# Modulation sums of the first feed-forward: one vector operation per eighth of a weight piece, fed by four one-chunk buffers

## The chip, the core and the metric

The kernel runs on one core of a Trainium2 chip. The core has a matrix engine (TensorE, PE in the profile; its weight loads are listed apart as PEld), a vector engine (VectorE, DVE), a scalar engine (ScalarE, ACT), a general engine (GpSimd, POOL) and a queue engine (SyncE, SP) that issues all DMAs of this kernel. They run side by side, each strictly in the order of its own instruction list, and wait for one another through semaphores. Data lie in SBUF and in HBM; products of PE land in PSUM, which has eight banks here, split in three pools ("a" four, "b" three, "c" one).

The metric is device time in microseconds (us), the median of several executions. The kernel before takes 3250.4 us (3247.34 to 3251.12, three runs).

## What is computed

The kernel is one layer of a diffusion backbone over 256 latent and 256 context tokens of width 2048. What matters here is the modulation and the first feed-forward step:

```
mod   = (silu(c)     @ w_ada + b_ada)      # 18432 columns for the latent stream
mod_c = (silu(c_ctx) @ w_ada + b_ada)      # and the same for the context stream
# x += 1/2 * gate * SwiGLU(modulate(RMSNorm(x)))  for both streams, width 5632 inside
h = _modulate(_rmsnorm(x, gain), m[:, 0], m[:, 1])
return x + HALF_STEP * m[:, 2] * _swiglu(h, w_gate, w_up, w_down)
```

After it come an input projection, a state-space scan, a Hyena branch, a merge and a second feed-forward, which use further columns of the same modulation. All of it is in float32; a product is made of three passes, with each operand split in a high part (the cast to the PE's own format) and a low part (the rest).

## The kernel before

The first feed-forward treats the 5632 inner columns in 22 blocks of 256. A block has six weight pieces of 1 MB: gate, up, gate, up (each 8 chunks of 128 rows by 256 columns, `gate_up`), then the down product of the block before in two pieces (`down` inside `ffn1`). Every piece costs PE 48 products of 128 x 512. `wpiece` prepares one: a DMA into `raw` (three buffers), a cast on ACT into the high part `wh` (two buffers), and two subtractions on DVE into the low part `wl` (two buffers). The `wh` of a piece can be written only when PE has done with the piece two earlier. The products of `down` go through PSUM into the running sums `xl` and `xc` by two DVE operations for each of 16 tiles (`evac1`), and between them stands the chain SiLU on ACT (`sil`, one buffer), product on DVE, cast on ACT (`ah`), rest on DVE (`al`).

Beside this work the kernel makes the remaining modulation, which needs 28 column groups of 512 (numbers 8 to 35). DVE does it: `ada_vec` multiplies a chunk of 128 x 512 of `w_ada` by one activation per row and adds it to an accumulator `ac`, once for each stream for the groups 8 to 19 (two-stream part) and once only for the groups 20 to 35 (one-stream part). Whenever two accumulators are full, PE sums them over the rows (`adacc`), ACT copies the sum (`adsb`), and after the last sum of a group PE transposes it (`adtp`) and DVE writes `modT`. As soon as the gate columns are there, `residual` adds the gated sums to the original `x` and `ctx`, which are read again. `s5_tables` makes tables for the scan in the same time, mostly on POOL, with transposes and small products on PE (`wtp`, `kp`) and DMAs out on SP.

`background` hands this work out: at each of the 132 weight pieces `step` pulls twice from the modulation and once from the tables. Chunks come in pairs, 512 KB per DMA into one of two buffers `raw2`, so that a pull issues four DVE operations in the two-stream part and two in the one-stream part. The kernel's text only names the dependences; a list scheduler then sets the order of each engine's instructions, by the place in the text and by when it takes inputs to be there. `issue_after` and the like give it a further order between two instructions, without a wait on the chip.

Of the kernel before, what the change touches and what calls it, by code (L numbers as in the profile page):

```python
# [19 lines left out]
P = 128  # L20
# [108 lines left out]
def _body(tc, nc, I, out, dbg, es):  # L129
# [36 lines left out]


    extra = []
    npiece, last = [0], [None]

    def wpiece(src, a, b):
        raw = wp.tile([P, 2048], F32, name="raw", tag="raw", bufs=3)
        last[0] = sync.dma_start(raw.rearrange("p (a b) -> p a b", a=a), src)
        npiece[0] += 1
        pl = extra[0] if extra and npiece[0] % 3 == 0 else wp
        H = pl.tile([P, 2048], FR, name="wh", tag="wh")
        act.copy(H, raw)  # L177
        L = pl.tile([P, 2048], FR, name="wl", tag="wl")
        for i in range(2):
            hs = slice(1024 * i, 1024 * i + 1024)  # L180
            dve.tensor_tensor(L[:, hs], raw[:, hs], H[:, hs].bitcast(F32), ALU.subtract)  # L181
        return (H.rearrange("p (a b) -> p a b", a=a), L.rearrange("p (a b) -> p a b", a=a))

    newest = [None]
# [36 lines left out]
    def ada_pe(nt, ap_):  # L221
# [16 lines left out]
            dve.tensor_tensor(modT[:, nt * 4:nt * 4 + 4, :], ps, PT[:, b0:b0 + 4].unsqueeze(2).to_broadcast([P, 4, 2]), ALU.add)  # L238
        yield

    def ada_vec(nts, ap_):


        ns = 2 if nts[0] < 20 else 1
        sb = ap_.tile([P, 512], F32, name="adsb", tag="adsb", bufs=1)
        per = 4 // ns
        acc = []
        for i, nt in enumerate(nts):
            new = [ap_.tile([P, 512], F32, name="ac", tag=f"ac{(i + s) % 2 if ns == 1 else s}", bufs=1) for s in range(ns)]
            for q in range(8):  # L250
                raw = ap_.tile([P, 2, 512], F32, name="raw2", tag="raw2", bufs=2)
                sync.dma_start(raw, w_ada[q * 256:(q + 1) * 256, nt * 512:(nt + 1) * 512].rearrange("(k p) n -> p k n", p=P))
                for g in range(2):
                    k = q * 2 + g
                    for s in range(ns):
                        if k == 0:
                            dve.tensor_scalar(new[s], raw[:, g], S32[:, k, s:s + 1], None, op0=ALU.mult)
                        else:
                            dve.scalar_tensor_tensor(new[s], raw[:, g], S32[:, k, s:s + 1], new[s], op0=ALU.mult, op1=ALU.add)  # L259
                yield  # L260
            acc += new
            if len(acc) < 2:
                continue

            ps = pc.tile([P, 512], F32, name="adacc", tag="c")
            r0 = 32 * (i * ns + ns - 2)
# [3 lines left out]
            act.copy(sb[r0:r0 + 64, :], ps[r0:r0 + 64, :])  # L270
            acc = []
        assert len(nts) == per
        tp = pc.tile([P, 4, P], F32, name="adtp", tag="c")
        for m in range(4):
            pe.transpose(tp[:, m, :], sb[:, m * P:(m + 1) * P], ident)

        m0 = nts[0] * 4
        b0 = col["b_ada"] + m0
        tv = tp.rearrange("p m (i s r) -> p m i s r", i=per, s=ns)
        for s in range(ns):  # L280
            dve.tensor_tensor(modT[:, m0:m0 + 4 * per, s].rearrange("p (i m) -> p m i", i=per), tv[:, :, :, s, 0],
                              PT[:, b0:b0 + 4 * per].rearrange("p (i m) -> p m i", i=per), ALU.add)
        yield

    def ada_rest(ap_):
        for nt in range(8, 20, 2):
            yield from ada_vec([nt, nt + 1], ap_)
            if nt == 10:
                gate_cols(0, 0.5)
                yield from residual(ap_)  # L290
        for nt in range(20, 36, 4):
            yield from ada_vec(list(range(nt, nt + 4)), ap_)

# [145 lines left out]
    def ffn1(fp, mm, evac, fill, begun):  # L439

        fill = iter(fill)

        def step():
            next(fill, None)

        wd = I["ffn_w_down"][0, 0]

        def hidden(b):
            if b == 0:
                gen, banks, pieces = begun  # L450
                for _ in range(pieces):
                    step()
            else:
                banks = []
                gen = gate_up(0, b, mm, banks)
            for piece in gen:
                if piece:
                    step()
            pg, pu = banks
            res = []  # L460
            for m in range(2):
# [10 lines left out]
        def down(b, a):  # L472
            for dh in range(2):
                H, L = wpiece(wd[b * 256:(b + 1) * 256, dh * 1024:(dh + 1) * 1024].rearrange("(k p) n -> p k n", p=P), 2, 1024)
                step()
# [479 lines left out]

    fp_cm, fp = open_pool("ffn1", side="right")

    for tag, shape, bufs in (("wg", [P, 1152], 2), ("raw2", [P, 1024], 2), ("ac0", [P, 512], 1), ("ac1", [P, 512], 1),
                             ("adsb", [P, 512], 1), ("bc_", [P, 512], 1), ("pq_", [P, 360], 1), ("ta", [P, 288], 1),
                             ("tb", [P, 288], 1), ("lag0", [P, 240], 1), ("lag1", [P, 240], 1)):  # L960
        fp.tile(shape, F32, name="slot", tag=tag, bufs=bufs)
# [14 lines left out]
    state = {}  # L976

    def residual(tp):
        for i in range(KD // 2):
            t = tp.tile([P, 2, 512], F32, name="raw2", tag="raw2", bufs=2)  # L980
            for s, nm in ((0, "t_x"), (1, "t_ctx")):
                sync.dma_start(t[:, :, s * SEQ:(s + 1) * SEQ], I[nm][i * 256:(i + 1) * 256, :].rearrange("(k p) n -> p k n", p=P))
            yield
            for k in range(2):
                dc = 2 * i + k
                assert state[dc] == "sum"
                for s, x in ((0, xl[dc]), (1, xc[dc])):
                    dve.scalar_tensor_tensor(x, x, gate[0][:, dc, s:s + 1], t[:, k, s * SEQ:(s + 1) * SEQ], op0=ALU.mult, op1=ALU.add)
                state[dc] = "gated"
            yield  # L990

    def background():

        ada, tab = ada_rest(fp), s5_tables(fp)
        while True:
            n = sum(next(ada, 0) is None for _ in range(2))
            n += next(tab, 0) is None
            if not n:
                return
            yield  # L1000
    rest = background()
    ffn1(fp, mm1, evac1, rest, (first, banks, 4))
    for _ in rest:
        pass
    scale_cols(1)
    gate_cols(1, 1.0)
    scale_cols(2)
# [369 lines left out]
```

## Time and profile before

| | |
|---|---|
| runs, median (lowest to highest) | 3250.4 us (3247.34 to 3251.12) |
| profiled execution: time, span | 3250.28 us, 3248.5 us |
| busy: PE, PEld, DVE | 3134.8 (97%), 2556.9 (79%), 2336.7 us (72%) |
| busy: ACT, POOL | 1104.8 (34%), 533.4 us (16%) |
| granted PE clock, mean | 0.985 |
| first product of the feed-forward to its last | 126.16 to 1721.6 us |

Busy shares are over the whole span. The first feed-forward fills about half of it; the rest is not touched by the change. PE is in the list as busy nearly always, but matmuls overlap: one lasts 0.39 us and the next starts 0.23 us after it, so that a gap in PE's list is shorter than the time that was lost. A row of a timeline gives the start, the length, the engine and line, what is written and read, and how often; in brackets the idle time of the engine before it and what ended it.

### The profile page before, as it was taken

How to read it: one execution, taken by the hardware profiler on the slowest of the kernel's cores; microseconds unless marked ns; L12 is line 12 of the kernel's file. 1: busy time of each engine (PE TensorE's matmuls, PEld its weight loads, DVE VectorE, ACT ScalarE, POOL GpSimd, SP SyncE). 2: the span in 40 equal slices, each digit the busy share in tenths (PEclk: the TensorE clock that was granted, in tenths of full speed). 3: DMA queues.
4: the chain of work that ended last, by engine and by line, in shares of the span. 5: the costliest groups of instructions: out<-in, count | busy, mean ns of one | idle time of the engine just before them, and what ended most of it. 6: DMA issues, size and time to landing. Idle time of an engine off the chain costs nothing.

```text
span 3248.5 us, 43933 instructions
## 1 busy us (share of the span) xinstructions
PE 3134.8 (97%) x17182; PEld 2556.9 (79%) x17182; DVE 2336.7 (72%) x3840; ACT 1104.8 (34%) x1474; POOL 533.4 (16%) x588
## 2 busy tenths in 40 slices
PE   7999999999999999999999899999999999999997
PEld 2477787777778878888888877788888888888886
DVE  5588787887766866677556478488877667766677
ACT  4323222222122211222225433545555444344443
POOL 1162352505143341000001040011100000000000
PEclk9999999999999999999999999999999999999999
DMA  9776465565556665866234667855665555555553
GB/s 302 269 245 210 162 198 172 178 196 181 183 186 216 215 198 170 253 211 218 97 94 121 164 223 240 268 177 184 205 204 165 188 186 192 181 188 187 187 190 104
DMA packets 479383, 625.98 MB, mean 193 GB/s; under 512 B 39399, under 2 KB 352328, under 8 KB 478920
## 3 DMA queue, kind: packets, MB, share of 16 engines
q1 hardware_dynamic: 479176, 623.17, 59.7%
q8 instruction: 136, 2.23, 0.3%
q14 instruction: 71, 0.58, 0.1%
HBM read 588.61 MB, written 38.70 MB: 193 GB/s over the span
## 4 chain that ended last, share of the span: by engine, by line
PE 79%; DVE 10%; DMA 6%; issue 2%; ACT 2%; POOL 1%; SPq 0%; DVEq 0%; POOLq 0%; ACTq 0%
PE prj L197 8%; PE pu L197 5%; PE pg L197 5%; PE pd L197 5%; PE pg L189 4%; PE pu L189 4%; PE pu L187 4%; PE pg L188 4%; PE pg L187 4%; PE pd L187 4%; PE pu L188 4%; PE pd L188 4%; PE pd L189 4%; PE prj L199 4%; DMA raw<-in_w_ada_dram 3%; DVE wl L181 3%
## 5 line engine op out<-in xcount | busy, mean ns | idle before, releaser
L181 DVE TENSOR_TENSOR wl<-raw,wh 128x1024 fp32r<-128x1024 f32 x736 | 900.3, 1263 | 365.2 <-ACT wh L177 363.9
L177 ACT CAST wh<-raw 128x2048 fp32r<-128x2048 f32 x368 | 702.9, 1910 | 1108.1 <-PE pd L188 312.4
L259 DVE SCALAR_TENSOR_TENSOR ac<-raw,S,ac 128x512 f32<-128x512 f32 x600 | 474.1, 820 | 143.6 <-DMA raw<-in_w_ada_dram 138.4
L197 PE MATMUL prj<-h,wh 128*128 128x512 f32 x896 | 322.7, 406 | 0.0
L187 PE MATMUL pd<-ah,wh 128*128 128x512 f32 x704 | 280.8, 400 | 16.1 <-ACT sil L465 10.4
L189 PE MATMUL pu<-h1H,wl 128*128 128x512 f32 x704 | 278.0, 399 | 7.5 <-DVE wl L181 7.5
L187 PE MATMUL pu<-h1H,wh 128*128 128x512 f32 x704 | 280.1, 399 | 0.0
L188 PE MATMUL pu<-h1L,wh 128*128 128x512 f32 x704 | 279.2, 397 | 0.0
L188 PE MATMUL pd<-al,wh 128*128 128x512 f32 x704 | 277.9, 395 | 0.0
L188 PE MATMUL pg<-h1L,wh 128*128 128x512 f32 x704 | 276.3, 393 | 0.9 <-DVE h1L L365 0.9
L187 PE MATMUL pg<-h1H,wh 128*128 128x512 f32 x704 | 275.2, 393 | 1.3 <-ACT wh L177 1.3
L189 PE MATMUL pd<-ah,wl 128*128 128x512 f32 x704 | 276.4, 395 | 0.0
L189 PE MATMUL pg<-h1H,wl 128*128 128x512 f32 x704 | 273.5, 393 | 2.2 <-DVE wl L181 2.2
L199 PE MATMUL prj<-h,wl 128*128 128x256 f32 x840 | 237.5, 290 | 7.2 <-DVE wl L181 7.1
L197 PE MATMUL pg<-h,wh 128*128 128x512 f32 x672 | 240.4, 398 | 4.0 <-DVE nt L511 3.4
L197 PE MATMUL pd<-ahl,wh 128*128 128x512 f32 x704 | 241.9, 397 | 2.3 <-DVE xl L536 1.7
L197 PE MATMUL pu<-h,wh 128*128 128x512 f32 x672 | 241.1, 396 | 0.0
L197 PEld LDWEIGHTS prj<-h,wh 128*128 128x128 f32 x896 | 169.7, 193 | 35.7 <-DVE h L365 0.3
L199 PE MATMUL pu<-h,wl 128*128 128x256 f32 x630 | 177.0, 281 | 0.0
L971 DVE SCALAR_TENSOR_TENSOR xl<-pd,gate,xl 128x256 f32<-128x256 f32 x314 | 149.1, 475 | 38.6 <-PE pd L189 38.2
L187 PEld LDWEIGHTS pd<-ah,wh 128*128 128x128 f32 x704 | 133.5, 190 | 55.1 <-ACT sil L465 13.3
L199 PEld LDWEIGHTS prj<-h,wl 128*128 128x128 f32 x840 | 162.4, 194 | 15.7 <-DVE wl L181 10.7
(457 smaller groups left out, 5776.7 us busy)
## 6 DMA issues: line engine op xcount, KB each, us to landing
raw<-in_w_ada_dram SPq DMA_DIRECT2D x224, 512.0 KB, 4.3
raw<-in_ffn_w_gate_dram SPq DMA_DIRECT2D x88, 1024.0 KB, 5.1
raw<-in_ffn_w_up_dram SPq DMA_DIRECT2D x88, 1024.0 KB, 5.1
raw<-in_ffn_w_down_dram SPq DMA_DIRECT2D x88, 1024.0 KB, 5.5
raw<-in_w_in_dram SPq DMA_DIRECT2D x64, 1024.0 KB, 6.2
raw<-in_w_ada_dram SPq DMA_DIRECT2D x32, 1024.0 KB, 5.8
raw<-in_w_pa_dram SPq DMA_DIRECT2D x16, 1024.0 KB, 5.4
raw<-in_w_out_dram SPq DMA_DIRECT2D x16, 1024.0 KB, 5.3
```

Source lines behind the costliest of these rows:

```text
L177: act.copy(H, raw)
L181: dve.tensor_tensor(L[:, hs], raw[:, hs], H[:, hs].bitcast(F32), ALU.subtract)
L187: pe.matmul(ps, H, xH, start=first, stop=False)
L188: pe.matmul(ps, H, xL, start=False, stop=False)
L189: mm = pe.matmul(ps, L, xH, start=False, stop=last)
L197: pe.matmul(ps.rearrange("p (a n) -> p a n", a=2), H, x, start=first, stop=last)
L199: pe.matmul(ps[:, SEQ:], L, x[:, 1], start=False, stop=False)
L259: dve.scalar_tensor_tensor(new[s], raw[:, g], S32[:, k, s:s + 1], new[s], op0=ALU.mult, op1=ALU.add)
L971: dve.scalar_tensor_tensor(x, p_, gate[0][:, dc, s:s + 1], x, op0=ALU.mult, op1=ALU.add)
```

## The change

The chunks of `w_ada` (and of `x` and `ctx`) are fetched singly, 256 KB into one of four buffers of half the size. `fetch` takes the next entry of a list `todo` and is called right behind the last operation that reads a buffer. `ada_vec` now yields after every DVE operation. A new `fine` takes one of them after each chunk of a gate or up piece, eight per piece, 32 per block, and gives each an order (without a wait) behind the newest weight product that was written down. The 21 blocks with such pieces have 672 places, and there are 384 + 32 + 256 operations. At down pieces no modulation operation is taken. The sums over rows (`ada_sum`) are taken once a block at the second down piece, behind the newest product. The tables are still pulled once per piece.

```diff
-            for q in range(8):
-                raw = ap_.tile([P, 2, 512], F32, name="raw2", tag="raw2", bufs=2)
-                sync.dma_start(raw, w_ada[q * 256:(q + 1) * 256, nt * 512:(nt + 1) * 512].rearrange("(k p) n -> p k n", p=P))
-                for g in range(2):
...
-                yield
+            for k in range(KD):
+                raw = loaded.pop(0)
+                for s in range(ns):
+                    if k == 0:
+                        dve.tensor_scalar(new[s], raw, S32[:, k, s:s + 1], None, op0=ALU.mult)
+                    else:
+                        dve.scalar_tensor_tensor(new[s], raw, S32[:, k, s:s + 1], new[s], op0=ALU.mult, op1=ALU.add)
+                    if s == ns - 1:
+                        fetch(ap_)
+                        if k == KD - 1:
+                            acc = acc + new
+                            if len(acc) == 2:
+                                sums.append((nts, ns, i, acc, sb))
+                                acc = []
+                    yield
...
+    def fetch(ap_):
+
+        if todo:
+            t = ap_.tile([P, 512], F32, name="raw2", tag="raw2", bufs=4)
+            kind, i, k = todo.pop(0)
+            if kind == "w":
+                sync.dma_start(t, w_ada[k * P:(k + 1) * P, i * 512:(i + 1) * 512])
+            else:
+                for s, nm in ((0, "t_x"), (1, "t_ctx")):
+                    sync.dma_start(t[:, s * SEQ:(s + 1) * SEQ], I[nm][k * P:(k + 1) * P, :])
+            loaded.append(t)
...
+    def ada_sum():
...
+        with tc.issue_after(newest[0]):
             mm = pe.matmul(ps[r0 + 32:r0 + 64, :], ones32, acc[1], start=True, stop=True)
...
             for piece in gen:
                 if piece:
-                    step()
+                    step(f"g{n}")
+                    n += 1
+                else:
+                    fine()
...
-        while True:
-            n = sum(next(ada, 0) is None for _ in range(2))
-            n += next(tab, 0) is None
...
+    def background(kind):
+
+
+        next(tab, None)
+        if kind == "d1":
+            ada_sum()
+
+    def fine():
+
+        traced = tc.nc.cur_bb.bb.instructions
+        n = len(traced)
+        next(ada, None)
+        for i in traced[n:]:
+            if i.engine != newest[0].engine and "DMA" not in type(i).__name__.upper():
+                tc.add_manual_dep(i, newest[0].name, mybir.DependencyInfo(mybir.DependencyClass.NoSync, mybir.DependencyReason.DATA), reason="pace")
```

Two places show what it does to the order. The first is DVE around the 54th weight piece, an up piece, the second piece of its block: `xl` and `xc` are the sums that `evac1` writes, `ac` the modulation, `wl` the low part of that piece. Before:

```order
L971 SCALAR_TENSOR_TENSOR xl_94<-pd,gate_2864,xl_94 128x256
L971 SCALAR_TENSOR_TENSOR xc_101<-pd,gate_2864,xc_101 128x256
L259 SCALAR_TENSOR_TENSOR ac<-raw_6098,S_90,ac 128x512 x3
L259 SCALAR_TENSOR_TENSOR ac<-raw_6104,S_90,ac 128x512
L971 SCALAR_TENSOR_TENSOR xl_94<-pd,gate_2864,xl_94 128x256
L971 SCALAR_TENSOR_TENSOR xc_101<-pd,gate_2864,xc_101 128x256
L259 SCALAR_TENSOR_TENSOR ac<-raw_6104,S_90,ac 128x512 x2
L971 SCALAR_TENSOR_TENSOR xl_94<-pd,gate_2864,xl_94 128x256
L971 SCALAR_TENSOR_TENSOR xc_101<-pd,gate_2864,xc_101 128x256
L259 SCALAR_TENSOR_TENSOR ac<-raw_6104,S_90,ac 128x512
L259 SCALAR_TENSOR_TENSOR ac<-raw_6165,S_90,ac 128x512
L181 TENSOR_TENSOR wl<-raw,wh 128x1024 x2
```

And in the changed kernel, where line 999 is the old line 971 and lines 267 and 269 the old lines 257 and 259:

```order
L999 SCALAR_TENSOR_TENSOR xl_94<-pd,gate_3845,xl_94 128x256
L999 SCALAR_TENSOR_TENSOR xc_101<-pd,gate_3845,xc_101 128x256
L267 TENSOR_SCALAR ac<-raw_5775,S_90 128x512
L269 SCALAR_TENSOR_TENSOR ac<-raw_5791,S_90,ac 128x512
L999 SCALAR_TENSOR_TENSOR xl_94<-pd,gate_3845,xl_94 128x256
L999 SCALAR_TENSOR_TENSOR xc_101<-pd,gate_3845,xc_101 128x256
L269 SCALAR_TENSOR_TENSOR ac<-raw_5791,S_90,ac 128x512
L269 SCALAR_TENSOR_TENSOR ac<-raw_5807,S_90,ac 128x512
L999 SCALAR_TENSOR_TENSOR xl_94<-pd,gate_3845,xl_94 128x256
L999 SCALAR_TENSOR_TENSOR xc_101<-pd,gate_3845,xc_101 128x256
L269 SCALAR_TENSOR_TENSOR ac<-raw_5807,S_90,ac 128x512
L181 TENSOR_TENSOR wl<-raw,wh 128x1024 x2
```

From the `wl` of the piece before to this one, DVE had 12 modulation operations and has 6; the writes of `xl` and `xc` among them are the same.

The second place is PE, at the first sum over rows. Before, it stands inside an up piece:

```order
L187 MATMUL pu<-h1H_1023,wh 128x512
L188 MATMUL pu<-h1L_1024,wh 128x512
L189 MATMUL pu<-h1H_1023,wl 128x512
L187 MATMUL pu<-h1H_1023,wh 128x512
L267 MATMUL adacc<-ac,ones_77 32x512
L269 MATMUL adacc<-ac,ones_77 32x512
L188 MATMUL pu<-h1L_1024,wh 128x512
L189 MATMUL pu<-h1H_1023,wl 128x512
```

In the changed kernel, with every line one or some twenty further down, it stands inside the second down piece of the block after:

```order
L188 MATMUL pd<-ah,wh 128x512
L189 MATMUL pd<-al,wh 128x512
L190 MATMUL pd<-ah,wl 128x512
L188 MATMUL pd<-ah,wh 128x512
L189 MATMUL pd<-al,wh 128x512
L287 MATMUL adacc<-ac,ones_77 32x512
L289 MATMUL adacc<-ac,ones_77 32x512
L190 MATMUL pd<-ah,wl 128x512
```

The accumulators `ac` that it reads are filled by the end of the last up piece ahead of it.

## Rows read from the trace of the kernel before

**Rows 1.** Three stretches: length; busy PE, PEld, DVE, ACT, POOL; clock, DMA share, GB/s

```profile
170.00:250.00 80.00, 72.63 (x333) 56.22 (x332) 70.87 (x82) 24.41 (x34) 50.34 (x50) 0.96 0.69 221
250.00:1300.00 1050.00, 1023.15 (x4792) 805.67 (x4792) 804.03 (x1223) 233.20 (x241) 358.02 (x430) 0.99 0.59 190
1300.00:1500.00 200.00, 200.00 (x899) 160.68 (x898) 145.65 (x231) 42.62 (x35) 0.00 (x0) 1.00 0.73 228
```

**Rows 2.** Who PE waited for, 170 to 1700: us in total, times, longest

```profile
PE pd L187 <- ACT sil L465: 10.4, 4, 3.8
PE pu L189 <- DVE wl L181: 7.5, 3, 4.0
PE wtp L914 <- POOL win L623: 4.9, 4, 2.1
PE adacc L267 <- DVE ac L259: 4.4, 1, 4.4
```

**Rows 3.** The same stretches view, by tile: wh, wl, wtp, kp, adacc

```profile
170.00:1700.00 1530.00, 1278.97 (x4090) 768.00 (x4090) 319.20 (x254) 244.28 (x128) 0.99 0.59 188
170.00:1700.00 1530.00, 798.85 (x2046) 386.24 (x2045) 319.20 (x254) 0.99 0.59 188
170.00:1700.00 1530.00, 20.78 (x128) 15.88 (x128) 18.63 (x32) 0.99 0.59 188
170.00:1700.00 1530.00, 21.10 (x512) 11.99 (x512) 2.65 (x16) 8.21 (x32) 0.99 0.59 188
170.00:1700.00 1530.00, 25.03 (x80) 3.34 (x80) 0.00 (x0) 11.61 (x20) 0.99 0.59 188
```

**Rows 4.** Timeline of PE at four table transposes

```profile
609.50 0.39 PE L189 MATMUL pu<-h1H,wl 128*128 128x512 f32 x1
...
610.09 0.48 PE L187 MATMUL pd<-ah,wh 128*128 128x512 f32 x1
```

**Rows 5.** Timeline of PE at the 54th piece

```profile
790.48 0.39 PE L189 MATMUL pd<-ah,wl 128*128 128x512 f32 x1
...
793.23 0.40 PE L189 MATMUL pg<-h1H,wl 128*128 128x512 f32 x1
...
794.13 0.51 PE L187 MATMUL pu<-h1H,wh 128*128 128x512 f32 x1
...
797.80 0.74 PE L189 MATMUL pu<-h1H,wl 128*128 128x512 f32 x2 [2.46 <-DVE wl L181]
```

**Rows 6.** Timeline of ACT there

```profile
790.68 1.92 ACT L177 CAST wh<-raw 128x2048 fp32r<-128x2048 f32 x1 [11.11 <-PE pd L188]
```

**Rows 7.** Timeline of DVE there

```profile
795.37 0.82 DVE L259 SCALAR_TENSOR_TENSOR ac<-raw,S,ac 128x512 f32<-128x512 f32 x1 [1.59 <-DMA raw<-in_w_ada_dram]
796.11 3.20 DVE L181 TENSOR_TENSOR wl<-raw,wh 128x1024 fp32r<-128x1024 f32 x2
```

**Rows 8.** DVE's groups, 250 to 1300: busy, mean ns, idle before

```profile
L259 DVE SCALAR_TENSOR_TENSOR ac<-raw,S,ac 128x512 f32<-128x512 f32 x454 | 355.1, 816 | 97.3 <-DMA raw<-in_w_ada_dram 94.4
L181 DVE TENSOR_TENSOR wl<-raw,wh 128x1024 fp32r<-128x1024 f32 x170 | 217.3, 1318 | 44.0 <-ACT wh L177 44.0
```

**Rows 9.** DVE's groups, 1300 to 1500

```profile
L259 DVE SCALAR_TENSOR_TENSOR ac<-raw,S,ac 128x512 f32<-128x512 f32 x80 | 59.9, 748 | 32.9 <-DMA raw<-in_w_ada_dram 31.2
L181 DVE TENSOR_TENSOR wl<-raw,wh 128x1024 fp32r<-128x1024 f32 x36 | 42.4, 1218 | 4.2 <-ACT wh L177 4.1
L971 DVE SCALAR_TENSOR_TENSOR xl<-pd,gate,xl 128x256 f32<-128x256 f32 x47 | 22.4, 476 | 3.2 <-PE pd L189 2.9
L468 DVE TENSOR_TENSOR al<-sil,ah 128x512 fp32r<-128x512 f32 x6 | 4.1, 684 | 0.5 <-ACT ah L467 0.5
```

**Rows 10.** DMA issues: count, KB each, median us to landing

```profile
raw<-in_w_ada_dram SPq DMA_DIRECT2D x224, 512.0 KB, 4.3
raw<-in_t_x_dram SPq DMA_DIRECT2D x8, 256.0 KB, 3.5
raw<-in_t_ctx_dram SPq DMA_DIRECT2D x8, 256.0 KB, 5.6
```

More of the change, by code (lines that the diff above doesn't have):

```diff
@@ L168, in _body @@
     extra = []
-    npiece, last = [0], [None]
+    npiece, last, lastL = [0], [None], [None]
     def wpiece(src, a, b):
@@ L239, in ada_pe @@
         yield
+    todo, loaded, sums = [], [], []
+    def fetch(ap_):
[8 more added lines that the diff above has]
+            loaded.append(t)
     def ada_vec(nts, ap_):
@@ L249, in ada_vec @@
             new = [ap_.tile([P, 512], F32, name="ac", tag=f"ac{(i + s) % 2 if ns == 1 else s}", bufs=1) for s in range(ns)]
-            for q in range(8):
-                raw = ap_.tile([P, 2, 512], F32, name="raw2", tag="raw2", bufs=2)
-                sync.dma_start(raw, w_ada[q * 256:(q + 1) * 256, nt * 512:(nt + 1) * 512].rearrange("(k p) n -> p k n", p=P))
-                for g in range(2):
[L254 to L259, printed above, removed]
-                yield
[L261 to L266, printed above, removed]
+            for k in range(KD):
[14 more added lines that the diff above has]
+    def ada_sum():
+        if not sums:
+            return
+        nts, ns, i, acc, sb = sums.pop(0)
+        ps = pc.tile([P, 512], F32, name="adacc", tag="c")
+        r0 = 32 * (i * ns + ns - 2)
+        with tc.issue_after(newest[0]):
             mm = pe.matmul(ps[r0 + 32:r0 + 64, :], ones32, acc[1], start=True, stop=True)
@@ L282, in ada_vec, with ada_rest @@
                               PT[:, b0:b0 + 4 * per].rearrange("p (i m) -> p m i", i=per), ALU.add)
+    def ada_rest(ap_):
+        todo.extend(("w", nt, k) for nt in range(8, 12) for k in range(KD))
+        todo.extend(("x", 0, k) for k in range(KD))
+        todo.extend(("w", nt, k) for nt in range(12, 36) for k in range(KD))
+        for _ in range(4):
+            fetch(ap_)
         yield
-    def ada_rest(ap_):
-        for nt in range(8, 20, 2):
+        for nt in (8, 10):
             yield from ada_vec([nt, nt + 1], ap_)
-            if nt == 10:
-                gate_cols(0, 0.5)
-                yield from residual(ap_)
+        assert not sums
+        gate_cols(0, 0.5)
+        yield from residual(ap_)
+        for nt in range(12, 20, 2):
+            yield from ada_vec([nt, nt + 1], ap_)
         for nt in range(20, 36, 4):
@@ L437, in gate_up, with ffn1 @@
                     yield False
[L439 to L444, printed above, removed]
+    def ffn1(fp, mm, evac, step, fine, begun):
         wd = I["ffn_w_down"][0, 0]
@@ L451, in hidden @@
                 for _ in range(pieces):
-                    step()
+                    step("g0")
             else:
@@ L474, in down @@
                 H, L = wpiece(wd[b * 256:(b + 1) * 256, dh * 1024:(dh + 1) * 1024].rearrange("(k p) n -> p k n", p=P), 2, 1024)
-                step()
+                step(f"d{dh}")
                 for dc in range(8):
@@ L978, in residual @@
     def residual(tp):
[L979 to L994, printed above, removed]
-        while True:
-            n = sum(next(ada, 0) is None for _ in range(2))
-            n += next(tab, 0) is None
[L998 to L1003, printed above, removed]
-        pass
+        for dc in range(KD):
+            t = loaded.pop(0)
+            assert state[dc] == "sum"
+            for s, x in ((0, xl[dc]), (1, xc[dc])):
+                dve.scalar_tensor_tensor(x, x, gate[0][:, dc, s:s + 1], t[:, s * SEQ:(s + 1) * SEQ], op0=ALU.mult, op1=ALU.add)
+                if s:
+                    state[dc] = "gated"
+                    fetch(tp)
+                yield
+    ada, tab = ada_rest(fp), s5_tables(fp)
+    next(ada)
+    def background(kind):
[9 more added lines that the diff above has]
+                tc.add_manual_dep(i, newest[0].name, mybir.DependencyInfo(mybir.DependencyClass.NoSync, mybir.DependencyReason.DATA), reason="pace")
+    ffn1(fp, mm1, evac1, background, fine, (first, banks, 4))
+    for _ in tab:
+        pass
+    for _ in ada:
+        pass
+    assert not sums and not todo and not loaded
     scale_cols(1)
```

14 lines of the change are left out of this document (8 added, 6 removed).

## The prediction

> **What bounds the kernel now.** I read three views, in this order. First the engines' busy time by stretch: from 170 to 1300 us PE lacks 34 us of being full, and its granted clock is under 1.00; from 1300 on it lacks nothing, at full clock [rows 1]. So the feed-forward is bound by PE, and what can be won lies before 1300. Next the waits of PE: nearly all are for SiLU on ACT, for `wl` on DVE, for the tables of POOL, and once for the accumulators of the modulation [rows 2]. Last the timeline at one of these waits, to see what DVE did instead.
>
> How much is lost in all? PE's list hides part of a gap, so I count products. Twelve of them take 793.23 - 790.48 = 2.75 us, 0.229 us each [rows 5]. From 170 to 1700 there are 4090 + 2046 = 6136 [rows 3], 1406 us. Beside them stand the sums over rows with 25.0 us, the tables' products with 21.1 us, and 128 transposes [rows 3] in fours; four cost 610.09 - 609.50 - 0.23 = 0.36 us [rows 4], so 11.5 us, and the ten fours for the modulation 3.6 us more. That makes 1468 of 1530 us: **62 us are lost**, by gaps and by the slow clock behind them.
>
> The 54th piece shows how. PE ends its last down product near 790.7 and wants the first `wl` product of that piece four products behind 794.13, at about 794.8; it gets it at 797.80 [rows 5]. The cast started the moment PE let go of the buffer and ended at 792.6 [rows 6]. DVE started `wl` at 796.11 only, because it was busy with modulation operations, the last of them late by a DMA [rows 7]. With a free DVE `wl` would have been there at 792.6 + 2 x 1.2 to 1.6 us [rows 7, 9], 795 to 795.8. So DVE's queue made 2 of the 3 us, and the rest is PE's own order: only 12 products stand there between the last down product and the up piece.
>
> **The change, part by part.**
>
> *Fewer modulation operations per block in the two-stream part.* A block has 288 products, 66.0 us; with tables and one sum some 69 us. DVE's part of it, before: 6 steps x 2 pulls x 4 = 48 operations of 0.816 us, 39.2 us, 12 `wl` halves of 1.318 us, 15.8 us [rows 8], 32 writes of the sums of 0.476 us, 15.2 us, and the four of the SiLU chain of about 0.68 us, 2.7 us [rows 9]: 72.9 us. DVE is overfull, and it falls on the down pieces: there 8 operations are added to 16 writes and a `wl`, 16.8 us of work in an 11 us piece. After: 32 operations, 26.1 us, so 59.8 us of 69, and all in the up and gate pieces (8 x 0.816 + 2.6 = 9.2 us of 11.0); a down piece keeps 7.6 + 2.6 = 10.2 us and the chain. No piece is far over its length, and each `wl` may be some 4 us late before PE waits. The DVE operations are the same 672, at the same price.
>
> *The place of the `wl` that is late most.* In the new order one modulation operation stands between the last write of a down tile and the `wl` of the second piece of a block, not a pile. PE's order moves with it: between the last down product and the first product of that piece I count 8 to 44 products in the 20 blocks before, 12 at the one shown, and 29 to 44 after, mostly 37. Cast and `wl` need 1.9 + 2.4 to 3.2 us, 19 to 22 products; 37 products are 8.5 us. Of the waits for `wl` and SiLU (7.5 + 10.4 us in the two largest rows [rows 2]), I let 3 us of the SiLU kind stand, since that chain still passes through one buffer and DVE's queue.
>
> *The sums over rows at the second down piece.* The one long wait, 4.4 us [rows 2], stood in an up piece with the accumulator just being filled. It goes: the accumulator is now full a piece earlier. The 20 sums cost PE the same. `modT` comes up to a block later; nothing in the feed-forward but the residual waits for it, and that starts in a later block with its own order.
>
> *One-stream part: more, and smaller.* There a step had 4 operations, a block 24; now 32: 23.9 + 14.6 + 15.2 + 2.7 = 56.4 us [rows 9] of 67.4 us for a block without tables. It fits, if the chunks come in time.
>
> *The DMAs.* 240 more issues on SP, 40 a block with the weights; what they cost SP lies beside its waits. The question is the landing. In the one-stream part each operation uses up a chunk. Four are loaded; the fifth in a run waits until the first one's buffer is filled again, L + 0.1 us after release, less the three operations between, 2.24 us. A block has five runs longer than four, so DVE waits 5 x (L - 2.1). What is L? The trace has 256 KB loads at 3.5 and, as the second of two, 5.6 us, and the 512 KB chunks at 4.3 us [rows 10]. Half a chunk should not be later than a whole; I take 3.9, midway from 3.5 to 4.3, which gives 9 us and 65.4 of 67.4 us: no loss, little to spare. At 3.5 it is 63.4; the limit is L = 4.3; at 5.6 it is 73.9, 6.5 us too much in each of eight blocks, 52 us. For the small side speaks that in 1300 to 1500 DVE did 80 of these and waited 31 us for their DMAs [rows 9] while PE lost nothing [rows 1]; the change asks for 95 in as long.
>
> The Trainium skill speaks against this part: "DMA: Bandwidth & Descriptors", section "Rules for kernel authors", wants at least 1 MiB in a DMA for the full bandwidth, and its fit for another issuing path (2.0 us + size / 436 GB/s) gives 2.6 us for 256 KB and 3.2 us for 512 KB as an estimate. By the rule the halves waste bandwidth, which is the second rival below; by the fit L would be under 4.3 us and nothing would be lost. The trace lies above the fit (4.3 us for 512 KB), so the measured rows decide.
>
> *What stays.* The gaps in the first block but for the sum, 7.4 - 4.4 = 3 us [rows 1, 2]; the waits for POOL's tables, 4.9 us [rows 2], since their order is as before; the 3 us of SiLU; and 3 us of slow clock behind these. 14 us of 62. **The sum:** the profiled execution took 3250.3 us (its span 3248.5, and about 2 around it), on the median of the runs, 3250.4; less 48 us it is 3202 us. With all 62 us gone it would be 3188.
>
> **Rivals.**
>
> *Chunks a little late (3222 us).* L lies between 4.3 and 5.4 in the one-stream part. At 4.8 DVE waits 13.5 us a block, 2.5 too many, 20 us in eight blocks. For it: refills queue behind weight pieces of four times their size. Against it: PE full in 1300 to 1500 with nearly this rate.
>
> *DMA becomes the bound of the one-stream part (3290 us, slower).* In a gate or up piece 1 MB of weights and eight chunks of 256 KB fall due within 11 us, 286 GB/s; the trace's 228 GB/s at a share of 0.73 [rows 1] put the full rate at 312. Refills then queue for one another: at L = 6.5 DVE waits 22 us, a block takes 78.4, 11 too much, 88 us in eight blocks, less the 48 won. From L = 5.4 on the loss is over the gain. Against it: the down pieces ask for 1 MB only and the buffers fill there, so that a block needs 14.7 MB in 67 us, 218 GB/s.
>
> *The order does not reach the waits (3246 us).* Nothing holds DVE at these places on the chip: the order is only one of its list. If the waits came from weights that land late or from POOL's stores holding up SP's queue, all but the sum's 4.4 us would stay. Against it: at the 54th piece cast and weights were there and DVE was not [rows 6, 7].
>
> **How the numbers follow.** Forecast 0.68, from 3186 to 3215 us; chunks a little late 0.15, 3215 to 3243; no effect 0.09; DMA bound 0.08. What a measurement can tell from no change is about 0.2%, 6.5 us, so faster means under 3244: 0.68 + 0.15 = 0.83; the same 0.09; slower 0.08. The range from 3186 to 3238 leaves out these 0.17 and a little of the second case.
>
> **What would show it.** Right: PE's waits for `wl` on DVE and for the accumulators gone from its list, clock 1.00 nearly throughout 250 to 1500, DVE busy at an even 75 to 85% there, feed-forward ending near 1674 instead of 1721.6. In the one-stream part DVE's idle time before line 269 should be some 9 us a block, with DMAs as releaser. Wrong: that idle time above 11 us a block with PE waiting for `wl` behind it (the DMA rivals), or the same gaps of PE with DVE idle before a `wl` whose cast is late (the third).

## The result, and the profile after

The changed kernel takes **3213.3 us** (median of four, 3211.95 to 3214.61) against 3249.5 in the same comparison: ratio 0.9892, 95% interval 0.9878 to 0.9905. That is 36 us less where 48 were forecast, 11 us above the predicted 3202 and inside the likeliest case's own range. The last product of the feed-forward ends at 1683.9 us; 1674 was forecast, and before it was 1721.6.

The stretches of [rows 1], now in the changed kernel:

```profile
170.00:250.00 80.00, 75.02 (x348) 58.77 (x347) 58.55 (x66) 27.08 (x42) 50.31 (x55) 0.98 0.67 217
250.00:1300.00 1050.00, 1049.07 (x5012) 836.77 (x5012) 785.98 (x1218) 241.82 (x241) 345.01 (x426) 1.00 0.57 184
1300.00:1500.00 200.00, 196.78 (x853) 159.12 (x852) 146.00 (x222) 39.89 (x31) 0.00 (x0) 0.99 0.71 229
```

From 250 to 1300 PE lacks 0.9 us of being full, before 26.9, at clock 1.00. But from 1300 to 1500, where it lacked nothing, it now lacks 3.2. The waits of PE from 170 to 1680, against [rows 2]:

```profile
PE pd L188 <- DVE sil L494: 4.9, 2, 3.2
PE pd L188 <- ACT sil L493: 3.7, 3, 1.8
PE wtp L942 <- POOL win L651: 2.5, 2, 1.8
PE kp L969 <- POOL gt L957: 1.6, 1, 1.6
...
PE pg L190 <- DVE wl L181: 0.4, 1, 0.4
```

The waits for the accumulators are gone, those for `wl` are down to one of 0.4 us, those for SiLU are not gone. What it costs, and where, shows in the lengths of the blocks. The table takes, from PE's timeline, the start of the first product of blocks 0, 10 and 14 (288 products a block) and the end of the last product. The times are medians; the blocks are those of one execution each, the profiled one, which lies up to 4 us from the median and in e5 6.7 us below it (3223.2, the four executions from 3223 to 3236). The two-stream groups of the kernel before end near block 10, those of the changed kernel at block 14.

| kernel | runs, us (ratio) | blocks 0 to 9 | 10 to 13 | 14 to 21 |
|---|---|---|---|---|
| before | 3249.5 | 757.9 | 285.5 | 552.1 |
| changed | 3213.3 (0.9892) | 717.7 | 279.3 | 560.9 |
| e1 no order | 3209.5 (0.9876) | 726.8 | 280.3 | 549.2 |
| e2 pairs | 3239.7 (0.9966) | 717.9 | 279.3 | 587.3 |
| e3 six buffers | 3204.2 (0.9857) | 717.2 | 279.3 | 548.7 |
| e4 half the loads | 3203.8 (0.9859) | 717.4 | 279.3 | 548.8 |
| e5 rate only | 3229.9 (0.9932) | 729.0 | 279.3 | 564.5 |
| e6 buffers only | 3239.2 (0.9960) | 746.3 | 284.3 | 547.8 |
| e7 sums at once | 3213.9 (0.9887) | 717.5 | 279.8 | 558.3 |
| e8 six, tables + 2 | 3210.4 (0.9871) | 712.7 | 279.4 | 562.8 |
| e9 order in the first part | 3199.6 (0.9845) | 717.4 | 279.3 | 547.9 |
| e10 e9, tables + 6 | 3195.6 (0.9832) | 709.0 | 279.3 | 551.2 |

The changed kernel wins 46.4 us in the first 14 blocks (3.8 of them three sums over rows, of 1.25 us each by [rows 3], that it makes later) and loses 8.8 in the last eight; e3, e4 and e9 show 12 there to be avoidable. How it loses them, on DVE at the largest of four such places:

```profile
1347.95 3.11 DVE L269 SCALAR_TENSOR_TENSOR ac<-raw,S,ac 128x512 f32<-128x512 f32 x4 [3.14 <-DMA raw<-in_w_ada_dram]
1350.98 2.35 DVE L181 TENSOR_TENSOR wl<-raw,wh 128x1024 fp32r<-128x1024 f32 x2
1353.25 3.11 DVE L269 SCALAR_TENSOR_TENSOR ac<-raw,S,ac 128x512 f32<-128x512 f32 x4
1360.50 0.75 DVE L269 SCALAR_TENSOR_TENSOR ac<-raw,S,ac 128x512 f32<-128x512 f32 x1 [4.14 <-DMA raw<-in_w_ada_dram]
1361.17 0.68 DVE L494 TENSOR_TENSOR sil<-sil,pu 128x512 f32<-128x512 f32 x1
```

Four chunks are used in a run, the fifth is not there, and behind the fifth stands the SiLU product. PE has done its last down product that can go without it:

```profile
1358.29 0.40 PE L190 MATMUL pd<-ah,wl 128*128 128x512 f32 x1
1361.90 0.51 PE L188 MATMUL pd<-ah,wh 128*128 128x512 f32 x1 [3.22 <-DVE sil L494]
```

Behind this gap PE's granted clock was 0.60 for 4 us, near the lower of its two levels (1.2 of 2.4 GHz), with the products 0.43 us apart instead of 0.23. So the four waits, 7.6 us in all, cost more than their length:

```profile
1361.90:1366.00 4.10, 4.10 (x11) 3.28 (x12) 4.10 (x7) 1.06 (x2) 0.00 (x0) 0.60 0.23 64
```

Why the fifth is late, in SP's queue:

```profile
1353.43 0.38 SPq L173 DMA_DIRECT2D raw<-in_ffn_w_up_dram  x1
1354.02 2.69 SPq L250 DMA_DIRECT2D raw<-in_w_ada_dram  x4
```

The refill is issued 0.6 us behind a weight piece of 1 MB. The issues of 1352 to 1357, of 1361 to 1362, when no weight piece stands ahead, and of 1300 to 1500 (count, size, median to landing):

```profile
raw<-in_w_ada_dram SPq DMA_DIRECT2D x4, 256.0 KB, 6.1
```

```profile
raw<-in_w_ada_dram SPq DMA_DIRECT2D x1, 256.0 KB, 2.7
```

```profile
raw<-in_w_ada_dram SPq DMA_DIRECT2D x96, 256.0 KB, 4.9
```

2.7 us alone (one load), 6.1 behind the weights, 4.9 at the median; I had taken 3.9.

### The profile page after: what moved, and what is told of

Same layout as the page of the kernel before. It is cut to its first block, busy times and chain, and to the rows that moved or that the text cites. A ratio compares the mean times of both kernels' runs of the same rounds, so it can differ in the third digit from the quotient of the medians.

```text
span 3212.7 us, 44551 instructions
## 1 busy us (share of the span) xinstructions
PE 3117.8 (97%) x17182; PEld 2551.6 (79%) x17182; DVE 2321.9 (72%) x3840; ACT 1104.0 (34%) x1474; POOL 518.4 (16%) x588
## 4 chain that ended last, share of the span: by engine, by line
PE 80%; DVE 8%; DMA 7%; issue 2%; POOL 1%; ACT 1%; SPq 0%; DVEq 0%; POOLq 0%; ACTq 0%
PE prj L198 8%; PE pg L198 5%; PE pu L198 5%; PE pd L198 5%; PE pd L188 5%; PE pd L189 5%; PE pd L190 5%; DMA raw<-in_w_ada_dram 4%; PE pg L190 4%; PE pg L189 4%; PE pg L188 4%; PE pu L189 4%; PE pu L188 4%; PE pu L190 4%; PE prj L200 4%; DVE wl L181 3%
## 5 line engine op out<-in xcount | busy, mean ns | idle before, releaser
L269 DVE SCALAR_TENSOR_TENSOR ac<-raw,S,ac 128x512 f32<-128x512 f32 x600 | 461.0, 804 | 112.0 <-DMA raw<-in_w_ada_dram 106.6
L999 DVE SCALAR_TENSOR_TENSOR xl<-pd,gate,xl 128x256 f32<-128x256 f32 x288 | 137.0, 476 | 60.1 <-PE pd L190 59.7
L200 PE MATMUL pg<-h,wl 128*128 128x256 f32 x630 | 174.8, 283 | 0.0
```

What stands on the lines that cost most here:

```text
L200: pe.matmul(ps[:, SEQ:], L, x[:, 1], start=False, stop=False)
L269: dve.scalar_tensor_tensor(new[s], raw, S32[:, k, s:s + 1], new[s], op0=ALU.mult, op1=ALU.add)
L999: dve.scalar_tensor_tensor(x, p_, gate[0][:, dc, s:s + 1], x, op0=ALU.mult, op1=ALU.add)
```

## The experiments

**e1, without the order.**

```diff
-        for i in traced[n:]:
-            if i.engine != newest[0].engine and "DMA" not in type(i).__name__.upper():
-                tc.add_manual_dep(i, newest[0].name, ...)
```

> The changed kernel without the order behind the newest weight product; one operation per eighth, the four one-chunk buffers and the place of the sums stay. Theory (the gain comes from where the modulation operations stand on VectorE, and the order alone puts them there): the scheduler heaps them up in the second down piece and the first gate piece again, by its order up to 18.2 us of VectorE work per 11 us piece where the changed kernel has 13.6 at most, and 26 to 31 products instead of 37 stand ahead of the second piece of a block; so waits of the matrix engine for `wl` and SiLU come back: 3225 to 3240 us, some 12 to 27 above the changed kernel. Rival (the buffers and the moved sums made the gain): 3213, within 4 us.

Measured 3209.5 us, ratio 0.9876 (0.9860 to 0.9893): no slower than the changed kernel. The theory is wrong as to the whole, and the table shows why: without the order 10 us are lost up to block 14 and 12 won behind it. The rival's number came out, but not its reason: up to block 14 the buffers (e2) and the moved sums (e7) are worth nothing. Of the 10 us, 6.6 come from one place in block 5, right behind the residual: a heap of eight operations ahead of the SiLU product, three more behind it, and then the writes of `xl` and `xc` that free PE's banks of PSUM. DVE there, and PE waiting for one of these writes:

```profile
519.49 5.39 DVE L269 SCALAR_TENSOR_TENSOR ac<-raw,S,ac 128x512 f32<-128x512 f32 x8
524.79 0.68 DVE L494 TENSOR_TENSOR sil<-sil,pu 128x512 f32<-128x512 f32 x1
```

```profile
533.80 0.47 PE L188 MATMUL pd<-ah,wh 128*128 128x512 f32 x1 [3.36 <-DVE xc L999]
```

PE's waits for `wl` are of 0.2 to 0.4 us here, although the scheduler puts up to 18 us of work between two of them and mostly only 26 to 31 products ahead of the second piece. At the lower rate these are enough; in block 5 of e5 even 7 stand there, and PE does not wait for that `wl`.

**e2, pairs.**

```diff
-            t = ap_.tile([P, 512], F32, name="raw2", tag="raw2", bufs=4)
             kind, i, k = todo.pop(0)
+            if k % 2 == 0:
+                return
+            t = ap_.tile([P, 2, 512], F32, name="raw2", tag="raw2", bufs=2)
...
-            loaded.append(t)
+            loaded.extend((t[:, 0], t[:, 1]))
```

> The changed kernel with two buffers of two chunks (512 KB a load) as before, refilled when the second chunk has been used; order, places and sums stay. Theory (the place of the operations makes the gain; the small buffers only matter in the one-stream part): the two-stream part ends where it does in the changed kernel, product 4608 at about 1264 us, within 3; in the one-stream part a pair is refilled later by one operation and lands later, so that VectorE waits more there: 20 us a block instead of 14, and the matrix engine loses some 10 us more: 3215 to 3230. Rival (single chunks made the gain in the two-stream part too): product 4608 later than 1275 and a time above 3230. Second rival (256 KB chunks were the worse ones, 512 KB saves queue time): 3200 to 3209.

Measured 3239.7 us (0.9955 to 0.9977). Up to block 14 the small buffers are worth nothing (997.2 against 997.0), as the theory said; behind it they are worth 26 us, more than expected, and the time lies above the range. Waits of PE from 170 to 1690 us, and DVE from 1300 to 1660:

```profile
PE pd L188 <- ACT sil L495: 19.2, 8, 2.9
```

```profile
L271 DVE SCALAR_TENSOR_TENSOR ac<-raw,S,ac 128x512 f32<-128x512 f32 x150 | 112.5, 750 | 85.0 <-DMA raw<-in_w_ada_dram 82.5
```

The changed kernel waited 68.1 us for chunks in that stretch. It is the same wait ahead of the same product, now in every one of the last eight blocks. A pair differs from two single chunks in its size and in when it is asked for again, and no run takes the two apart.

**e3, six buffers in the last blocks.**

```diff
+            j = (i - 26) * KD + k
+            if j >= 0 and j % 6 < 2:
+                t = ap_.tile([P, 1152], F32, name="raw2w", tag="wg", bufs=2)[:, :512]
+            else:
+                t = ap_.tile([P, 512], F32, name="raw2", tag="raw2", bufs=4)
...
             loaded.append(t)
+            if j in (0, 1):
+                fetch(ap_)
```

> The changed kernel with two more one-chunk buffers from column group 26 on (in the room of the tables' buffers, which are done by then), so six chunks are loaded ahead in the last five blocks. Theory (what the one-stream part loses is the fifth chunk in a run, late behind a weight piece, ahead of the SiLU product in VectorE's order): the four losses there, at 1358, 1500, 1634 and 1638 us of the changed kernel, with the half clock behind them about 11 us, go; 3201 to 3206, VectorE's idle time for chunks from 1350 on falls below 7 us a block from 14. Rival (the DMAs' rate is the limit there, so buffers only move the wait): 3211 to 3215 and the same idle time.

Measured 3204.2 us (0.9842 to 0.9871), feed-forward done at 1671.4 us. All four stalls are gone, and the time is in the range of the theory. DVE's wait for chunks from 1350 to 1600, the changed kernel and then this one:

```profile
L269 DVE SCALAR_TENSOR_TENSOR ac<-raw,S,ac 128x512 f32<-128x512 f32 x107 | 80.2, 750 | 42.5 <-DMA raw<-in_w_ada_dram 40.1 <-DVE ac L269 0.3
```

```profile
L275 DVE SCALAR_TENSOR_TENSOR ac<-raw,S,ac 128x512 f32<-128x512 f32 x71 | 53.2, 749 | 13.0 <-DMA raw<-in_w_ada_dram 11.4
...
L275 DVE SCALAR_TENSOR_TENSOR ac<-raw2w,S,ac 128x512 f32<-128x512 f32 x35 | 26.3, 750 | 5.1 <-DMA raw2w<-in_w_ada_dram 4.4
```

40.1 becomes 15.8 us at the same bytes, some 4 us a block. So it was the time to landing, which two more buffers cover, and not the rate of the DMAs: the rival of a DMA bound falls.

**e4, half the loads.**

```diff
             kind, i, k = todo.pop(0)
+            if i >= 20 and k % 2:
+                loaded.append(half[0])
+                return
```

> The changed kernel, with every chunk of the one-stream groups used twice and every second chunk of them not loaded (so the modulation of these groups is not the right one): half the bytes and half the loads of this kind, the same VectorE operations in the same order. Theory (late chunks make the loss in the one-stream part): product 4608 to the end of the feed-forward falls from 420 to some 407 us, 3199 to 3205 in all, and VectorE's wait for chunks nearly vanishes there. Rival (the loss is the order of the operations around the SiLU product, whatever the loads): 3211 to 3215 with the same waits for SiLU.

Measured 3203.8 us (0.9844 to 0.9873): the same as e3, with the operations where they were. DVE's operations on chunks from 1300 to 1660 then sit idle 3.9 us in all, and not for a DMA (71.4 us in the changed kernel):

```profile
L272 DVE SCALAR_TENSOR_TENSOR ac<-raw,S,ac 128x512 f32<-128x512 f32 x150 | 112.5, 750 | 3.9
```

Without late chunks the order costs nothing here, so they are the loss.

**e5, the rate, in the kernel before.**

```diff
                 if piece:
-                    step()
+                    step(8)
...
-            n = sum(next(ada, 0) is None for _ in range(2))
+            done, n = 0, 0
+            while done < places:
+                ops = next(ada, -1)
+                if ops == -1:
+                    break
+                done += ops
+                n += 1
             n += next(tab, 0) is None
```

(`ada` now yields the number of operations it issued; `places` is what `step` was given, none at down pieces.)

> The kernel before with one thing changed: the modulation is pulled in at gate and up pieces only, eight VectorE operations a piece, 32 a block in both parts (before: 48 a block in the two-stream part, 24 in the one-stream part). Pairs of 512 KB in two buffers, the sums over rows as soon as two accumulators are full, no order behind a product: all as before. Theory (what overfilled VectorE in the two-stream part was the rate, 73 us of work in a block of 69.6, and not the place within the block): the waits for `wl` and SiLU go there, product 4608 starts at about 1270 us (between 1260 and 1280) against 1316 before and 1264 in the changed kernel; in the one-stream part pairs lose as in the run with pairs, some 16 to 20 us; 3225 to 3242. Rival (single chunks or the moved sums are needed for it): product 4608 later than 1295 and 3245 or more.

Measured 3229.9 us (0.9910 to 0.9954). Block 14 starts 1008.3 us after block 0, so 35 of the 46 us come without the order, the small buffers and the moved sums, by this execution, the fastest of its four. Product 4608 starts at 1284, 4 us behind the range: block 5 is 9 us longer than in the changed kernel, at the same place as in e1, and blocks 14 and 15 lose 5 us each, as with pairs. The last eight blocks lose 16 us in all, as expected. What is left of PE's waits from 170 to 1690:

```profile
PE pd L187 <- ACT sil L465: 11.3, 6, 4.1
...
PE adacc L267 <- DVE ac L259: 1.2, 1, 1.2
PE pu L189 <- DVE wl L181: 0.4, 1, 0.4
```

The 7.5 us for `wl` of [rows 2] are 0.4, and the sums wait 1.2 us in all, though they stand as soon as two accumulators are full, as before. Two things change at once in e5, the number of operations in a block and that none is pulled at down pieces, and no run separates them. But the pile ahead of the `wl` of a block's second piece stays, 10 or 11 operations in most of the two-stream blocks where the kernel before had up to 12, and PE does not wait behind it.

**e6, the buffers alone, in the kernel before.**

```diff
+        for _ in range(8 if ops[0] < 416 else 4):
+            ops[0] += 1
+            next(ada, None)
         next(tab, None)
-        if kind == "d1":
-            ada_sum()
```

(against the changed kernel: no `fine`, the sums as soon as they are full, without an order)

> The kernel before with one thing changed: four one-chunk buffers for the two pairs. The modulation is pulled in at every piece as before, eight operations in the two-stream part and four in the one-stream part, and the sums stand where two accumulators are full, without an order. Theory (the rate made the two-stream loss): VectorE stays overfull there, product 4608 at 1305 us or later, the one-stream part loses nothing; 3238 to 3255. Rival (single chunks made the gain): product 4608 before 1280 and 3205 to 3225.

Measured 3239.2 us (0.9945 to 0.9976), with product 4608 at 1301, 4 us earlier than the theory allowed. The rate is not quite the old one: there the transposes and the loads for the residual used up pulls of their own, here they do not, so that blocks 2 to 8 have 50 modulation and residual operations each, in the kernel before 42. Block 10 starts 746.3 us after block 0, 12 earlier than before in spite of that and 29 later than in the changed kernel, and the accumulators' wait is there as before (the three largest of PE's waits from 170 to 1690):

```profile
PE pd L188 <- ACT sil L492: 7.8, 4, 3.5
PE wtp L941 <- POOL win L650: 7.0, 6, 1.8
PE adacc L288 <- DVE ac L269: 5.4, 2, 4.6
```

**e7, the sums at once.**

```diff
                             if len(acc) == 2:
                                 sums.append((nts, ns, i, acc, sb))
                                 acc = []
+                                ada_sum()
...
-        if kind == "d1":
-            ada_sum()
```

> The changed kernel with the sums over rows given to the matrix engine as soon as two accumulators are full (behind the newest product of that moment, the end of the last up piece) instead of at the second down piece. Theory (the sums cost only where the matrix engine waits for the last modulation operation, one such wait of 4.4 us before): most of the 20 sums now wait for VectorE's last operations by 0 to 2 us each, 5 to 20 us in all, PE's list names the accumulators as what it waits for; 3218 to 3233. Rival (the order leaves VectorE far enough ahead): 3211 to 3216, no such waits.

Measured 3213.9 us (0.9871 to 0.9904), the same as the changed kernel; up to the start of block 14 no sum waits. Three do later (waits of PE from 170 to 1700):

```profile
PE adacc L288 <- DVE ac L269: 6.9, 3, 3.9
```

The rival is right up to block 14: at the lower rate DVE is ahead. Behind it the sums do wait, and the time is the same in spite of it: over the whole the place of the sums is worth next to nothing.

**e8, the first tables' transposes two pieces later, with six buffers.**

```diff
                 yield
                 yield
+                if q == d == 0:
+                    yield
+                    yield
```

> The run with six buffers, and two pulls more between the first table's work on GpSimd and its transposes, so that the transposes stand two pieces later. Theory: the matrix engine's waits for the first tables, 4.6 us in the first full block of the feed-forward, go, with a little half clock behind them: 3 to 6 us below the run with six buffers (3204.2), 3198 to 3201. Rival (the work on GpSimd is late because its input is, and something else waits in the place): within 2 us of it.

Measured 3210.4 us (0.9856 to 0.9886), above both forecasts. The first blocks win 4.5 us, but not as expected: the first table's own transposes did not move and still wait 2.5 us. What is gone is 1.6 us of PE's wait for the first `kp`, and one table's 32 products `kp` (1.3 us by [rows 3]) now stand behind block 10. From block 14 to the end 14 us are lost, 13 of them in blocks 14 to 16. Of PE's waits from 170 to 1700, the three on DVE and ACT stand there:

```profile
PE kp L978 <- DVE lag L984: 3.1, 2, 2.1
PE pd L188 <- ACT sil L499: 2.9, 2, 1.6
PE pd L188 <- DVE sil L500: 2.7, 2, 2.4
PE wtp L951 <- POOL win L657: 2.5, 2, 1.8
```

On DVE it is again an operation on a late chunk with something that PE needs behind it, here at 1133 us `lag`, a small operation of the tables:

```profile
1133.39 3.12 DVE L275 SCALAR_TENSOR_TENSOR ac<-raw,S,ac 128x512 f32<-128x512 f32 x4 [4.63 <-DMA raw<-in_w_ada_dram]
1136.42 2.35 DVE L181 TENSOR_TENSOR wl<-raw,wh 128x1024 fp32r<-128x1024 f32 x2
1138.69 0.74 DVE L275 SCALAR_TENSOR_TENSOR ac<-raw,S,ac 128x512 f32<-128x512 f32 x1
1139.35 0.16 DVE L984 TENSOR_TENSOR lag<-lag,kp 128x16 f32<-128x16 f32 x1
```

The six buffers begin at group 26 only, behind these blocks. In e3 PE has no wait at all there; why the chunks come later in e8 is not shown. DVE's operations were slower too, from 250 to 1300 in e3 and in e8:

```profile
L275 DVE SCALAR_TENSOR_TENSOR ac<-raw,S,ac 128x512 f32<-128x512 f32 x420 | 317.9, 805 | 40.0 <-DMA raw<-in_w_ada_dram 37.9
```

```profile
L275 DVE SCALAR_TENSOR_TENSOR ac<-raw,S,ac 128x512 f32<-128x512 f32 x420 | 346.5, 873 | 50.6 <-DMA raw<-in_w_ada_dram 48.7
```

Every later table moved by two pieces within its block, and the modulation operations now run beside POOL more often. But that is not the loss: the slower operations stand before 1110 us (a mean of 807 ns in e3, 891 in e8), where blocks 2 to 13 take the same time in both; from 1110 to 1300, where the time is lost, the means are 798 and 797.

**e9, the order in the two-stream part only.**

```diff
         next(ada, None)
+        used[0] += 1
+        if used[0] > 416:
+            return
```

> The changed kernel with the order behind the newest product for the first 416 operations only, those of the two-stream part; in the one-stream part the scheduler places them as in the run without an order. Four one-chunk buffers as in the changed kernel. Theory (in the one-stream part the order put five chunk operations ahead of the SiLU product, of which the fifth waits for a chunk behind a weight piece; without it at most two stand there; in the two-stream part the order saves the 10 us by which the run without it was longer): block 14 starts about 997 us after block 0, the rest takes about 549 us; 3200 to 3205. Rival (the two parts are not separate, the one-stream stalls come from a buffer state that the two-stream part leaves): 3209 to 3215.

Measured **3199.6 us** (0.9831 to 0.9858), 0.4 below the range, block 14 at 996.7 and the rest 547.9: as forecast. DVE ahead of the SiLU product, in the block whose stall is shown above:

```profile
1344.02 2.35 DVE L181 TENSOR_TENSOR wl<-raw,wh 128x1024 fp32r<-128x1024 f32 x2
1346.29 1.53 DVE L269 SCALAR_TENSOR_TENSOR ac<-raw,S,ac 128x512 f32<-128x512 f32 x2
1350.13 0.69 DVE L494 TENSOR_TENSOR sil<-sil,pu 128x512 f32<-128x512 f32 x1 [2.31 <-PE pu L190]
```

Two chunk operations instead of five, and DVE waits for PE there, not PE for DVE.

**e10, the same with the tables one whole block later.** The edit of e8 with six yields for two, in e9.

> The run before this one, with six pulls more between the first table's work on GpSimd and its transposes, one block, so that every later table keeps its place within a block (two pulls more moved them, and VectorE's modulation operations then took 0.87 us instead of 0.80 beside GpSimd). Theory (the place within the block made that loss; the waits for the first table cost 4.5 us): 3 to 6 us below the run before this one, VectorE's operations at 0.80 us. Rival (tables that reach one block further into the one-stream part cost as much as in the run with two pulls): 2 to 8 us above it.

Measured **3195.6 us** (0.9818 to 0.9845), the best of all. DVE's operations are back at 805 ns, the waits for the first tables (5.2 us in e9) are gone. Of the 8.4 us won up to block 10, some 2 are only moved (8 transposes and 32 products `kp`, by [rows 3, 4]); at the end 3.3 are lost, 2.5 of them in block 16, where the tables now run a block longer. That the place within the block made e8's loss agrees with this; that the slower operations made it does not follow.

## Why the prediction was right, and what it had wrong

*The rate.* Right in its effect, and the largest part: with 32 operations a block, none pulled at down pieces, 35 of the 46 us come by themselves (e5). The sum behind it was too large. It took 48 operations a block and priced each by its length; the trace has 42 in blocks 2 to 8 with those of the residual, since a pull that ends with the transposes or only loads for the residual issues none, and in a run they follow one another closer than their length (eight in 5.4 us in e1, 0.67 us each, of a mean length of 750 ns). So DVE was not overfull as a whole. The stretches of blocks 2 to 8, before and changed:

```profile
289.90:810.40 520.50, 506.44 (x2378) 396.52 (x2376) 423.65 (x649) 111.31 (x108) 204.40 (x238) 0.98 0.57 182
286.30:773.70 487.40, 487.40 (x2334) 389.80 (x2333) 365.57 (x574) 109.49 (x105) 185.69 (x230) 1.00 0.53 174
```

Before, DVE is busy 60.5 us of a block of 74.4, 81%, changed 52.2 of 69.6, 75%. In the rest it waited itself, for chunks (31.5 us in the seven blocks) and for accumulators (19.5), which are late in turn. It was nearly full only where the operations pile up, as in block 1 with 66 of them (70.2 of 77.9 us), and in e6 with 50 a block (91%). So what PE feels is fewer operations, as many in every block, and not a block that was too short for all of them. I had the rate for the whole two-stream stretch; in the kernel before that ended near block 10. The gaps that follow, in blocks 10 and 14, are already of the other kind, a modulation operation late by its chunk, with the SiLU product behind it:

```profile
1197.70 0.75 DVE L259 SCALAR_TENSOR_TENSOR ac<-raw,S,ac 128x512 f32<-128x512 f32 x1 [2.32 <-DMA raw<-in_w_ada_dram]
1198.37 0.68 DVE L466 TENSOR_TENSOR sil<-sil,pu 128x512 f32<-128x512 f32 x1
```

*The place of the `wl` that is late most.* Wrong as a cause. The 37 products ahead of it did not matter: 26 to 31 (e1) do as well, since at the lower rate DVE comes to `wl` in time. What the order does bring is 10 us, two thirds of it at one place, behind one heap. (At the 54th piece the traces have 11 modulation operations and 12 writes before, 6 and 14 after.)

*The sums at the second down piece.* The 4.4 us went, but by the rate and not by the place: e7 puts the sums back and loses next to nothing up to block 14 (0.3 us); in e6, where the rate is high and the sums stand at once, they wait 5.4 us.

*One-stream part, the landing.* This is the term that was mis-sized. I took L = 3.9 us for all chunks and found a wait of 9 us a block, under the limit. Measured from 1300 to 1500 were 4.9 at the median and, on line 269, 43.1 us of waiting for chunks, some 14.5 a block:

```profile
L269 DVE SCALAR_TENSOR_TENSOR ac<-raw,S,ac 128x512 f32<-128x512 f32 x90 | 67.5, 750 | 44.9 <-DMA raw<-in_w_ada_dram 43.1
```

That is the rival "chunks a little late" at its 4.8, and above the 11 us a block that I had named as a sign of being wrong; but PE waited for SiLU behind it and not for `wl`, and it cost 12 us and not 20. The sum over a block was the wrong measure. DVE's own work is 51.8 us a block in blocks 18 to 20, not 56.4, so that 14.5 of waiting still fit into 67.4. PE pays only where the waiting stands ahead of the SiLU product. That happens in blocks 17, 19 and 21, where five operations and not four stand between the last `wl` and that product, and the order, which I had priced as a gain only, is what puts them there (e9).

The Trainium skill, "DMA: Bandwidth & Descriptors", section "Rules for kernel authors", wants at least 1 MiB a DMA for the maximum bandwidth, which speaks for larger loads; here the 512 KB pairs were the slower by 26 us in the last blocks (e2), where bandwidth was not the limit (e3). The same page's fit, given for DMAs issued from GpSimd (section "Anatomy of one DMA — SWDGE (gpsimd) path"), makes 2.6 us of 256 KB as an estimate, and the lone chunk took 2.7; the fit does not hold behind a weight piece, where it took 6.1.

*What stays.* For the tables 4.6 us of waits stayed where 4.9 were forecast, but that is partly luck: 2.5 of them are for the transposes (6.3 before, with a row that I left out) and 2.1 for the first `kp`, where there were none. For SiLU I let 3 us stand; 8.6 did, all of it in the last eight blocks.

*The rivals.* "The order does not reach the waits" fell, in that the waits went; but its reason, that the order holds nothing by itself, was near the truth: most of the gain comes without the order. The DMA bound fell by e3.

So the size came out short by the 12 us of late chunks. Of the three reasons given for the rest, one was right though its sum was not (the rate), and the other two, the place and the sums, owe their waits to it.

## What to carry to other kernels

Before placing background work, count it, in the block and in each piece of it, and read the engine's busy time beside the count: here some 42 operations a block, unevenly spread over the blocks, cost nearly 5 us a block in blocks 2 to 8, and 32 in every block next to nothing, while the order of the 32 decided over 10 us in one part and 12 in the other. A wait for a load costs by what is queued behind it, so look which instruction on the path stands behind the operation that waits, and keep no more operations ahead of that instruction than there are loaded buffers. Take the landing time of a small load from the place where it shares the queue with the large ones, not from a mean.

## What was not expected of the hardware

A VectorE operation of 128 x 512 takes 750 ns where GpSimd does nothing (1300 to 1660) and a mean of 805 or 873 where GpSimd works, by how the two happen to fall together: moving the tables by two pieces made that difference (e8), and with the tables moved by a whole block it is not there (e10). From 250 to 1300 those that no GpSimd instruction overlaps take at most 755 ns in both e3 and e8; 110 of the 420 in e3 are overlapped, 144 in e8, with means of 970 and 1118 ns. It cost no time where DVE had room. GpSimd pays as well: from 250 to 1300 its busy time was 344.5 us for 426 instructions in e3 and 380.3 for 430 in e8. The Trainium skill, "SBUF — State Buffer", section "SBUF: two separate sides", says that a VectorE operation with two inputs in SBUF and a GpSimd operation that reads SBUF share a pair of ports, which the one that starts first holds to its end. These operations have two such inputs and single ones took up to 1.3 us, so the traces agree; that moving a whole series of tables by two pieces is worth 29 us of VectorE's time in one stretch is not to be read from it.
